# Hybrid retention/DeltaNet/RG-LRU block: block transposes on VectorE with 128-byte runs to DRAM, retention states in four places, q norms by block sums

## Chip, cores and metric

One core of one Trainium2 chip. The metric is the device time of one execution in microseconds; every figure of before is from runs of the same kernel on the same inputs.

## The reference, cut to what matters

Two layers on one sequence of 1024 tokens, width 1024. Layer 0 mixes with four retention heads and four gated-DeltaNet heads; layer 1 with an RG-LRU; after each mixer comes a feed-forward block with a short convolution. The change is almost all in layer 0's mixer:

```python
q_r, k_r, v_r, g_r, q_d, k_d, v_d, g_d, b_d, a_d = jnp.split(hn @ w_in, split_at, axis=-1)
# retention, chunks of 128 tokens, head by head
scores = jnp.einsum('bhnid,bhnjd->bhnij', qc, kc) * dmask
kv = jnp.einsum('bhncd,bhncv->nbhdv', k_tail, vc)      # needs k and v token-major
s = s * chunk_decay + kv_n                             # the state, chunk after chunk
y = intra + q_decay @ s_prev ; y_r = _rms(y) * silu(g_r)
# DeltaNet: causal conv + silu, l2norm of q and k, triangular solve, then a scan over chunks
v_new = u_n - w_n @ s ; o = qd_n @ s + a_n @ v_new ; s = s * cd_n + kt_n.T @ v_new
y_d = rms_norm(y_d, out_gain) * silu(g_d)
h = h + concat(y_r, y_d) @ w_out
```

## The kernel before

Activations lie feature-major: 128 features on the partitions, the 1024 tokens along the row. A projection (`project`, `project_n`) is 2 halves of 512 tokens by 8 tiles of the contraction by 3 matmuls (`mm3`, lines 328 to 330: high by high, high by low and low by high parts of fp32 numbers). Each weight quarter is loaded on SyncE's queue (line 260), cast to its high part on ScalarE (line 270) and its low part taken on VectorE (line 271); a ring of 6 quarters runs ahead of TensorE. A half accumulates in one of four PSUM tiles tagged `pp`; VectorE empties it (`evac_r`, line 388, or `rot_head`'s `evac`, lines 1437 to 1440).

Around the projections the small chains are written as generators. `slot()` is called after each three matmuls of a projection, and every second slot takes one step of a lane: `gdn` (`gates`, `a_stage`, `subst`, `merge`, then `scan(n)` for the eight chunks) and `ret` (`ret_half`). `after(n, f)` puts f off by n slots. A scheduler then orders each engine's instructions in this order of writing, moving one ahead where by its own model an earlier one isn't ready; on the chip each engine, SyncE's queue too, runs its list strictly in order.

In layer 0's mixer (`_mix0`) the projections run: three k heads together, the gates, the fourth k head, four q heads (`conv_head("q", ...)`), four gates (`gate2`), four v heads, then for each retention head its q, k and v, then the last gates. What is needed token-major is turned by TensorE transposes of 128x128 blocks against `ident` into PSUM and copied from there:

- `scan`: v at line 1389, K at line 1397;
- `ret_half`: v at line 1459, k at line 1464, copied by ScalarE at lines 1461 and 1466;
- `normalise`: the output on its way back, in `post` at lines 1366 and 1367, eight slots later, with one store (line 1368).

`qnorm` sums the squares of q by matmuls with a column of ones (line 1345). `normalise` squares on ScalarE (1352), sums on VectorE (1354, 1358), takes the power on GpSimd (1359), multiplies on VectorE (1361). `ret_half`'s state alternates between two places `rs`: the update for chunk n+1 (line 1483) must wait until the output matmul of chunk n-1 (line 1478) has read the place, and stands between the output matmuls of neighbouring chunks.

In the feed-forward block, products 0 to 6 use seven operands; `store_parts` writes them to DRAM, as high and low parts (`p_dram`, "whole") or as plain numbers (`s_dram`) that `load_set` splits again (lines 840 and 841).

Of the kernel before, what the change touches and what calls it, by code (L numbers as in the profile page):

```python
# [103 lines left out]
class Block:  # L104
# [655 lines left out]
    def ffn(self, layer, gain):  # L760
# [3 lines left out]
        s_dram = self.tc.dram_tile([2, 4, 4, P, HALF], F32, name=f"sf_dram{layer}")  # L764
# [15 lines left out]
        place = {1: 0, 4: 1, 2: 2, 6: 3}  # L780
        whole = {0: 0, 1: 1, 3: 2, 5: 3}
        room = {}

        def store_parts(p, y, hi):
# [11 lines left out]
            def store_split(o, src, at):  # L796
                A.copy(halves(hi[:, at]), src)  # L797
                V.tensor_tensor(halves(lo[:, at]), src, f32(halves(hi[:, at])), ALU.subtract)
                for e, t in enumerate((hi, lo)):
                    nc.sync.dma_start(p_dram[c, whole[o], k % 4, e], f32(t[:, at]))  # L800
# [22 lines left out]
            store_split(5, v[:, :, 0], slice(HALF, T))  # L823

        def load_set(c, o):

            x = self.operand(o)
            if o in whole:
                for k in range(4):
                    for e in range(2):  # L830
                        nc.sync.dma_start(f32(x[:, :, 4 * e + k, :]), halves(p_dram[c, whole[o], k, e]))
# [120 lines left out]
    def rglru(self, gain):  # L952
# [5 lines left out]

        sm = lambda name: pool.tile([P, 8], F32, name=name)
# [12 lines left out]
        us = pool.tile([P, 8 * HALF], F32, name="us")  # L972
        xs = pool.tile([P, 4 * T], F32R, name="xs")
# [110 lines left out]
    def mix0(self, gain):  # L1084
        tc = self.tc
        self.q_dram = tc.dram_tile([NCH, P, HALF], F32, name="q_dram")
        self.v_dram = tc.dram_tile([NCH, P, HALF], F32, name="v_dram")
# [21 lines left out]
    def _mix0(self, room):  # L1109
# [89 lines left out]
        def conv_tail(kind, h, buf, dst):  # L1199
# [9 lines left out]
            return th  # L1209

# [131 lines left out]
        def qnorm(h, s):  # L1342
            p = self.pc()
            for n in range(NCH):
                PE.matmul(p[:, n:n + 1], s[:, n * P:(n + 1) * P], self.ones, start=True, stop=True)

            V.tensor_scalar(irho[:, h * NCH:(h + 1) * NCH], p[:, 0:NCH], 4.0 * EPS, 128.0 * EPS, ALU.add, ALU.mult)

        def normalise(o, eps, ydst, i):
# [13 lines left out]
            def post():  # L1363
                p = self.pc()
                for h in range(4):
                    PE.transpose(p[:, hs(h)], on[:, hs(h)], self.ident)
                A.copy(s, p)
                nc.sync.dma_start(ydst, ps4(s) if len(ydst.shape) == 3 else s)
            self.after(8, post)

        def scan(n):
# [4 lines left out]
            nc.sync.dma_start(v, self.v_dram[n])  # L1376
# [10 lines left out]
            pv = self.pc()  # L1387
            for h in range(NH):
                PE.transpose(pv[:, hs(h)], v[:, hs(h)], self.ident)
# [3 lines left out]
            yield  # L1393
            if n < NCH - 1:
                p = self.pc()
                for h in range(NH):
                    PE.transpose(p[:, hs(h)], K[h][:, cs], self.ident)
                kt = tmp2("kt")
                V.tensor_tensor(ps4(kt), ps4(p), bc_last(cn(ekt), P), ALU.mult)
            s0, s1 = S[n % 2], S[(n + 1) % 2]  # L1400
            if n > 0:
                p = self.pc()
                for h in range(NH):
                    PE.matmul(p[:, hs(h)], K[h][:, cs], s0[:, hs(h)], start=True, stop=True)
                for h in range(NH):
                    V.scalar_tensor_tensor(v[:, hs(h)], p[:, hs(h)], col(ck, h, n), v[:, hs(h)], ALU.mult, ALU.add)
# [22 lines left out]
            normalise(o, cn(irho), self.y_dram[4:8, :, cs].rearrange("h p c -> p h c"), 0)  # L1429


        def rot_head(ti):
# [3 lines left out]
            def evac(n, sl, ps):  # L1436
# [4 lines left out]
                G.tensor_tensor(r[:, sl], r[:, sl], t, ALU.add)  # L1441
            self.project(unit, evac)
            return r

        def ret_half(h, i, q, k, v):
# [11 lines left out]
            p = self.pc()  # L1457
            for c in range(4):
                PE.transpose(p[:, hs(c)], v[:, cs(c)], self.ident)
            vt = tmp2("rvt")  # L1460
            A.copy(vt, p)
            p = self.pc()
            for c in range(4):
                PE.transpose(p[:, hs(c)], k[:, cs(c)], self.ident)
            kt = tmp2("rkt")
            A.activation(kt, p, AF.Copy, scale=retc[:, 2 * HALF + h:2 * HALF + h + 1])
            yield
# [4 lines left out]
            yield from range(2)  # L1472
            o = self.pc()
            for c in range(4):
                n = n0 + c
                s0, s1 = rs[n % 2], rs[(n + 1) % 2]
                if n > 0:
                    PE.matmul(o[:, hs(c)], qd[:, hs(c)], s0, start=True, stop=False)
                PE.matmul(o[:, hs(c)], sc[:, hs(c)], vt[:, hs(c)], start=n == 0, stop=True)
# [4 lines left out]
            normalise(o, None, self.y_dram[h][:, sl], 1)  # L1484
# [10 lines left out]

        gdn = self.lane("gdn", 2, 0)
# [60 lines left out]
        for h in range(NH):  # L1557
# [5 lines left out]
            self.after(28, lambda h=h, q2=q2: qnorm(h, q2))  # L1563
# [3 lines left out]
        for h in range(NH):  # L1567
            v = conv_head("v", h, None)
            nc.sync.dma_start(self.v_dram[:, :, hs(h)].rearrange("n p c -> p n c"),
                              v.rearrange("p (n c) -> p n c", n=NCH))  # L1570
# [3 lines left out]
        retc = rest[:, 0:2 * HALF + 4]  # L1574
        rs = [rest[:, 2 * HALF + 4 + i * P:2 * HALF + 4 + (i + 1) * P] for i in range(2)]
        nc.scalar.dma_start(retc, I["retc"])
# [8 lines left out]
        for h in range(NH):  # L1585
            q = rot_head(h)
            k = rot_head(4 + h)
            unit = self.unit("mix_in", 8 + h)
            v = self.t()
            self.project(unit, self.evac_r(v))  # L1590
            ret += [ret_half(h, i, q, k, v) for i in range(2)]
# [117 lines left out]
```

## Time and profile before

| | us |
|---|---|
| median of 3 runs | 2199.09 (2198.58 to 2200.04) |
| the profiled execution | 2200.31 |
| its span, first to last instruction | 2198.5 |
| TensorE matmuls busy | 2176.4 (99%) |
| TensorE weight loads busy | 1819.5 (83%) |
| VectorE busy | 1696.0 (77%) |
| ScalarE busy | 1069.7 (49%) |

Layer 0's mixer fills about the first 510 us. In the views below, "PE" is TensorE, "PEld" its weight loads, "DVE" VectorE, "ACT" ScalarE, "POOL" GpSimd, "SPq" the queue of SyncE that issues nearly all transfers. A row of instruction groups has: line, engine, operation, output<-inputs, shape, count | busy us, mean ns of one | idle us just before, and what ended it. Matmuls overlap, so the mean of one is longer than its step, and busy is the union.

### The profile page before, as it was taken

What the parts mean: (1) busy time and instruction counts of PE and PEld (TensorE: products, weight loads), DVE (VectorE), ACT (ScalarE), POOL (GpSimd) and SP (SyncE); (2) the same over time, 40 slices, a digit from 0 to 9 for tenths busy, and PEclk for the clock granted to TensorE, in tenths of its full rate; (3) what the DMA queues carried; (4) which work ended last, traced back from release to release, by engine and by line L of the source; (5) the groups of instructions that cost most, each with busy time, mean ns of one, the idle gap of its engine ahead of it and who ended that gap; (6) DMA issues with size and microseconds to landing.
All of it is one profiled execution on the core that took longest, in us unless ns stands there. A gap on an engine that the chain in (4) does not pass through costs nothing.

```text
span 2198.5 us, 29909 instructions
## 1 busy us (share of the span) xinstructions
PE 2176.4 (99%) x10844; PEld 1819.5 (83%) x10844; DVE 1696.0 (77%) x2576; ACT 1069.7 (49%) x1712; POOL 80.8 (4%) x73
## 2 busy tenths in 40 slices
PE   9999999999999999999999999999999999999998
PEld 8887888887888888887888888888888888878888
DVE  6988766446899988987865677778999889878644
ACT  5334433124565555554323476765655555544321
POOL 0100111200000000000000000000000000000001
PEclk9999999999999999999999999999999999999999
DMA  4243424125234544438546211242245445375542
GB/s 173 81 141 99 128 83 145 57 79 175 63 120 167 179 153 157 163 111 287 197 160 201 82 53 63 85 147 73 101 165 171 148 173 177 115 271 178 190 165 77
DMA packets 203300, 305.34 MB, mean 139 GB/s; under 512 B 31728, under 2 KB 91408, under 8 KB 203152
## 3 DMA queue, kind: packets, MB, share of 16 engines
q1 hardware_dynamic: 202720, 301.85, 40.7%
q8 instruction: 85, 1.39, 0.3%
q10 hardware_dynamic: 432, 1.58, 0.2%
q14 instruction: 63, 0.52, 0.1%
HBM read 212.63 MB, written 90.72 MB: 138 GB/s over the span
## 4 chain that ended last, share of the span: by engine, by line
PE 89%; DMA 4%; DVE 4%; issue 2%; ACT 1%; POOL 1%; SPq 0%; POOLq 0%; DVEq 0%; ACTq 0%
PE ps L328 27%; PE ps L330 27%; PE ps L329 27%; DMA t<-sf_dram 1%; DMA t<-y_dram 1%; PE pc L433 1%; DMA s<-pf_dram 1%; DMA h<-in_xT_dram 0%; DVE wlo L271 0%; PE pc L448 0%; DVE l L1273 0%; DVE l L1271 0%; PE pc L328 0%; PE pc L330 0%; PE pc L329 0%
## 5 line engine op out<-in xcount | busy, mean ns | idle before, releaser
L328 PE MATMUL ps<-s,whi 128*128 128x512 f32 (+1 forms) x2792 | 1091.0, 392 | 3.9 <-ACT s L840 1.8
L329 PE MATMUL ps<-s,whi 128*128 128x512 f32 (+1 forms) x2792 | 1084.5, 388 | 1.0 <-DVE s L841 0.7
L330 PE MATMUL ps<-s,wlo 128*128 128x512 f32 (+1 forms) x2792 | 1083.9, 388 | 0.0
L270 ACT CAST whi<-raw 128x512 fp32r<-128x512 f32 (+1 forms) x612 | 371.5, 613 | 659.1 <-PE ps L329 515.6
L328 PEld LDWEIGHTS ps<-s,whi 128*128 128x128 f32 x2792 | 524.9, 188 | 112.5 <-ACT s L840 3.1
L330 PEld LDWEIGHTS ps<-s,wlo 128*128 128x128 f32 x2792 | 524.7, 188 | 108.1 <-DVE wlo L271 0.3
L329 PEld LDWEIGHTS ps<-s,whi 128*128 128x128 f32 x2792 | 525.2, 188 | 107.3 <-DVE s L841 1.8
L271 DVE TENSOR_TENSOR wlo<-raw,whi 128x512 fp32r<-128x512 f32 (+1 forms) x612 | 412.9, 680 | 60.8 <-ACT whi L270 57.2
L774 DVE SCALAR_TENSOR_TENSOR t<-halo,cols,t 128x1024 f32<-128x1024 f32 x176 | 222.1, 1282 | 4.8 <-ACT t L772 3.5
L747 DVE TENSOR_TENSOR halo<-ps,kept 128x512 f32<-128x512 f32 (+1 forms) x138 | 92.2, 668 | 75.5 <-PE ps L330 74.2
L757 DVE TENSOR_TENSOR h<-ps,h 128x512 f32<-128x512 f32 x112 | 77.4, 691 | 82.2 <-PE ps L330 81.9
L772 ACT ACTIVATE t<-halo,cols 128x1024 f32<-128x1024 f32 x88 | 109.7, 1246 | 16.9 <-DVE halo L747 11.6
L742 ACT COPY kept<-ps 128x512 f32<-128x512 f32 (+1 forms) x138 | 77.0, 558 | 13.3 <-PE ps L330 11.2
L498 DVE TENSOR_TENSOR h<-ps,h 128x512 f32<-128x512 f32 (+1 forms) x72 | 45.3, 631 | 43.3 <-PE ps L330 43.3
L438 POOL TENSOR_TENSOR rtok<-rtok,npow 128x4 f32<-128x4 f32 (+1 forms) x11 | 11.2, 1016 | 1722.3 <-DVE rtok L437 1668.7
L857 DVE TENSOR_TENSOR t<-t 128x1024 f32<-128x1024 f32 x44 | 53.7, 1221 | 0.0
L797 ACT CAST t<-t 128x512 fp32r<-128x512 f32 x64 | 38.1, 620 | 32.0 <-DVE t L857 30.7
L852 ACT ACTIVATE t<-t 128x1024 f32<-128x1024 f32 x44 | 46.8, 1063 | 10.1 <-DVE t L774 10.0
L416 ACT ACTIVATE t<-h 128x512 f32<-128x512 f32 (+1 forms) x49 | 27.2, 562 | 46.3 <-DVE h L498 41.5
L840 ACT CAST s<-t 128x512 fp32r<-128x512 f32 x48 | 29.5, 621 | 38.4 <-DMA t<-sf_dram 34.0
L328 PE MATMUL ps<-s,s 128*128 128x256 f32 (+1 forms) x144 | 46.2, 321 | 0.0
L329 PE MATMUL ps<-s,s 128*128 128x256 f32 (+1 forms) x144 | 45.8, 318 | 0.0
(293 smaller groups left out, 2074.5 us busy)
## 6 DMA issues: line engine op xcount, KB each, us to landing
raw<-in_ffn_up_dram SPq DMA_DIRECT2D x176, 256.0 KB, 2.7
s<-pf_dram SPq DMA_DIRECT2D x128, 256.0 KB, 5.3
pf_dram<-t SPq DMA_DIRECT2D x64, 256.0 KB, 2.6
pf_dram<-lo SPq DMA_DIRECT2D x64, 256.0 KB, 2.5
sf_dram<-t SPq DMA_DIRECT2D x64, 256.0 KB, 2.2
t<-sf_dram SPq DMA_DIRECT2D x64, 256.0 KB, 5.0
raw<-in_ffn_w_dram SPq DMA_DIRECT2D x64, 256.0 KB, 2.9
raw<-in_mix_in_dram SPq DMA_DIRECT2D x62, 256.0 KB, 2.9
```

Source lines behind the costliest of these rows:

```text
L270: self.nc.scalar.copy(hi[:, 0:w], raw[:, 0:w])
L271: eng.tensor_tensor(lo[:, 0:w], raw[:, 0:w], f32(hi[:, 0:w]), ALU.subtract)
L328: mm(ps, whi, xhi, start=start, stop=False)
L329: mm(ps, whi, xlo, start=False, stop=False)
L330: mm(ps, wlo, xhi, start=False, stop=stop)
L742: A.copy(kept[o], ps)
L747: V.tensor_tensor(dst(i, j), v(ps), v(kept[k]), ALU.add)
L757: V.tensor_tensor(h(*to[o]), ps.rearrange("p (h c) -> p h c", c=256), h(*to[o]), ALU.add)
L772: A.activation(t, buf[:, 2:2 + T], AF.Identity, scale=w(0), bias=self.col(f"ffn_cb{layer}", tile_i))
L774: V.scalar_tensor_tensor(t, buf[:, 2 + j:2 + j + T], w(j), t, ALU.mult, ALU.add)
L852: A.activation(tg, tg, AF.Silu)
L857: V.tensor_tensor(tg, tg, tv, ALU.mult)
```

## The change

1. `store_t`: VectorE transposes every 32x32 block of a tile into `room`, and four transfers write it to DRAM token-major, each of 32 partitions by 32 blocks by 32 numbers (1024 runs of 128 bytes for a 1024-token tile). Used for K and v of DeltaNet (4 + 4 tiles of 1024 tokens) and for k and v of retention (8 + 8 halves). `scan` loads K and v so turned, scales them and has one lane step less; `ret_half` finds its k and v in `rt`, loaded by `ret_load`.
2. `normalise` transposes blocks on VectorE at once, in place of `post`, and stores with 4 transfers (scan) or 16 (retention half).
3. Retention: order of units v, k, q; v goes from PSUM to a half tile; the states have four places and are all updated right after the `kv` matmuls, ahead of the output matmuls; `rt`'s second half lies in the tile `lo` of `parts`.
4. `qnorm`: block transpose of the squares, a sum on VectorE over 32 columns, four stores and four loads of single numbers through `qq_dram`, and a second sum, at once instead of 28 slots later.
5. Feed-forward: operand 5 of the first half of products (c = 0) goes to DRAM as plain numbers (one store for two, one load for two) and is split at `load_set`.
6. RG-LRU: `xs` and `us` are allocated ahead of the small columns.

```diff
-            o += [(("mix_in", i), 2) for i in (h, 4 + h, 8 + h)]
+            o += [(("mix_in", i), 2) for i in (8 + h, 4 + h, h)]
...
-        place = {1: 0, 4: 1, 2: 2, 6: 3}
-        whole = {0: 0, 1: 1, 3: 2, 5: 3}
+        place = {1: 0, 4: 1, 2: 2, 6: 3, 5: 4}
+        whole = [{0: 0, 1: 1, 3: 2}, {0: 0, 1: 1, 3: 2, 5: 3}]
...
+            if 5 in whole[c]:
+                store_split(5, v[:, :, 0], slice(HALF, T))
+            else:
+                nc.sync.dma_start(halves(s_dram[c, place[5], k % 4]), v[:, :, 0])
...
+        def store_t(dst, src, room):
+            V.transpose(room, src)
+            for a in range(4):
+                bs = slice(a * 32, (a + 1) * 32)
+                nc.sync.dma_start(dst[:, bs].rearrange("(b i) j -> i b j", i=32),
+                                  room[bs, :].rearrange("p (b j) -> p b j", j=32))
...
-        def qnorm(h, s):
-            p = self.pc()
-            for n in range(NCH):
-                PE.matmul(p[:, n:n + 1], s[:, n * P:(n + 1) * P], self.ones, start=True, stop=True)
+        def qnorm(h, s, room):
+            V.transpose(room, s)
+            V.tensor_reduce(q32, room.rearrange("p (b j) -> p b j", j=32), AX.X, ALU.add)
+            d = self.qq_dram[h]
+            for a in range(4):
+                nc.sync.dma_start(d[a].rearrange("(b i) -> i b", i=32), q32[a * 32:(a + 1) * 32, :])
+            for a in range(4):
+                nc.sync.dma_start(qx[:, a * NCH:(a + 1) * NCH], d[a].rearrange("(n p) -> p n", p=P))
+            V.tensor_reduce(rho, qx.rearrange("p (a n) -> p n a", a=4), AX.X, ALU.add)
...
-            def post():
-                p = self.pc()
-                for h in range(4):
-                    PE.transpose(p[:, hs(h)], on[:, hs(h)], self.ident)
-                A.copy(s, p)
-                nc.sync.dma_start(ydst, ps4(s) if len(ydst.shape) == 3 else s)
-            self.after(8, post)
+            V.transpose(s, on)
+            for a in range(4):
+                bs = slice(a * 32, (a + 1) * 32)
+                for d, c in ydst(a):
+                    nc.sync.dma_start(d, s[bs, c].rearrange("p (m j) -> p m j", j=32))
...
-            pv = self.pc()
-            for h in range(NH):
-                PE.transpose(pv[:, hs(h)], v[:, hs(h)], self.ident)
-            V.tensor_tensor(ps4(v), ps4(pv), bc_last(cn(cv), P), ALU.mult)
...
+                nc.sync.dma_start(kt, self.kt_dram[cs])
+                V.tensor_tensor(ps4(kt), ps4(kt), bc_last(cn(ekt), P), ALU.mult)
+            V.tensor_tensor(ps4(v), ps4(v), bc_last(cn(cv), P), ALU.mult)
...
+        def ret_load(h):
+            for i in range(2):
+                for e in range(2):
+                    nc.sync.dma_start(ps4(rt[i][e]),
+                                      self.rt_dram[e, h, i * HALF:(i + 1) * HALF].rearrange("(c p) d -> p c d", p=P))
+                nc.scalar.activation(rt[i][1], rt[i][1], AF.Copy, scale=ktail[:, h:h + 1])
...
-                s0, s1 = rs[n % 2], rs[(n + 1) % 2]
+                s0, s1 = rs[n % 4], rs[(n + 1) % 4]
...
-            self.after(28, lambda h=h, q2=q2: qnorm(h, q2))
+            qnorm(h, q2, blocks())
+            store_t(self.kt_dram[:, hs(h)], K[h], blocks())
...
+            self.project(self.unit("mix_in", 8 + h), evac)
+            k = rot_head(4 + h, self.rt_dram[1, h])
             q = rot_head(h)
+            ret_load(h)
+            ret += [ret_half(h, i, q, k) for i in range(2)]
```

More of the change, by code (lines that the diff above doesn't have):

```diff
@@ L799, in store_split @@
                 for e, t in enumerate((hi, lo)):
-                    nc.sync.dma_start(p_dram[c, whole[o], k % 4, e], f32(t[:, at]))
+                    nc.sync.dma_start(p_dram[c, whole[c][o], k % 4, e], f32(t[:, at]))
             store = lambda o, r: nc.sync.dma_start(s_dram[c, place[o], k % 4], r)
@@ L1456, in ret_half @@
             yield
[L1457 to L1467, printed above, removed]
+            vt, kt = rt[i]
             kv = self.pc()
@@ L1483, in ret_half @@
                     V.scalar_tensor_tensor(s1, s0, RET_CD[h], kv[:, hs(c)], ALU.mult, ALU.add)
-            normalise(o, None, self.y_dram[h][:, sl], 1)
+            yield from range(3)
+            o = self.pc()
+            for c in range(4):
+                n = n0 + c
+                if n > 0:
+                    PE.matmul(o[:, hs(c)], qd[:, hs(c)], rs[n % 4], start=True, stop=False)
+                PE.matmul(o[:, hs(c)], sc[:, hs(c)], vt[:, hs(c)], start=n == 0, stop=True)
+            y = self.y_dram[h].rearrange("(b i) t -> i b t", i=32)
+            normalise(o, None, lambda a: [(y[:, :, (n0 + c) * P + a * 32:(n0 + c) * P + (a + 1) * 32], hs(c))
+                                          for c in range(4)], 1)
         def together(*gens):
@@ L1494, in together @@
                 yield from range(2)
+        blocks = lambda: f32(self.parts.tile([P, T], F32R, tag="lo", name="lo"))
+        half = lambda: self.kept.tile([P, HALF], F32, tag="kept", name="kept")
         gdn = self.lane("gdn", 2, 0)
```

84 lines of the change are left out of this document (43 added, 41 removed).

## The prediction

> **What bounds the kernel now.** I read the page first: its busy times and the chain that ended last.
>
> ```profile
> span 2198.5 us, 29909 instructions
> PE 2176.4 (99%) x10844; PEld 1819.5 (83%) x10844; DVE 1696.0 (77%) x2576; ACT 1069.7 (49%) x1712; POOL 80.8 (4%) x73
> PE 89%; DMA 4%; DVE 4%; issue 2%; ACT 1%; POOL 1%; SPq 0%; POOLq 0%; DVEq 0%; ACTq 0%
> ```
>
> TensorE sets the end: it is busy 99% of the span and holds 89% of the chain. So work taken off TensorE comes off the time unless a new wait of TensorE eats it. Where that could be is seen by stretches of layer 0's mixer (us, then busy us and count of PE, PEld, DVE, ACT, POOL, then clock, DMA share, GB/s):
>
> ```profile
> 65.00:97.00 32.00, 32.00 (x163) 26.90 (x162) 29.56 (x65) 13.04 (x21) 1.46 (x3) 1.00 0.29 92
> 97.00:144.00 47.00, 47.00 (x248) 40.27 (x248) 41.05 (x106) 21.05 (x45) 9.37 (x4) 1.00 0.41 110
> 144.00:187.00 43.00, 43.00 (x199) 35.86 (x199) 38.79 (x88) 9.45 (x12) 0.00 (x0) 1.00 0.40 141
> 246.00:366.00 120.00, 117.36 (x780) 104.64 (x779) 80.23 (x165) 42.32 (x101) 23.62 (x19) 1.00 0.35 105
> 366.00:478.00 112.00, 110.79 (x614) 94.73 (x614) 52.05 (x94) 24.43 (x40) 24.75 (x19) 1.00 0.22 75
> ```
>
> VectorE is the second engine: 87 to 92% busy from 65 to 187 us (the q heads, the gates, the substitution), 67% in the scans (246 to 366), 46% in the later retention heads. The granted clock is 1.00 throughout, so a price in us holds.
>
> **What TensorE loses.** The removed groups, and one that is only moved (the last):
>
> ```profile
> L1366 PE MATMUL pc<-ident,l 128*128 128x128 f32 x64 | 9.6, 272 | 0.0
> L1459 PE MATMUL pc<-ident,t 128*128 128x128 f32 x32 | 4.8, 272 | 0.0
> L1464 PE MATMUL pc<-ident,t 128*128 128x128 f32 x32 | 4.8, 273 | 0.0
> L1389 PE MATMUL pc<-ident,l 128*128 128x128 f32 x32 | 4.8, 273 | 0.0
> L1397 PE MATMUL pc<-ident,h 128*128 128x128 f32 x28 | 4.2, 272 | 0.0
> L1345 PE MATMUL pc<-ones,l 128*128 128x1 f32 x64 | 7.4, 245 | 0.0
> L1478 PE MATMUL pc<-l 128*128 128x128 f32 x56 | 11.3, 284 | 2.2 <-DVE l L1483 2.2
> ```
>
> Their busy time adds up to 35.6 us, the upper end, since it counts pipeline tails that lie under neighbours. The steps between starts are in the timeline (start, us, instruction, idle before):
>
> ```profile
> 249.06 0.39 PE L330 MATMUL ps<-s,wlo 128*128 128x512 f32 x1
> 249.29 0.60 PE L1397 MATMUL pc<-ident,h 128*128 128x128 f32 x4
> 249.64 0.48 PE L328 MATMUL ps<-s,whi 128*128 128x512 f32 x1
> 249.96 0.39 PE L329 MATMUL ps<-s,whi 128*128 128x512 f32 x1
> 100.45 1.84 PE L1345 MATMUL pc<-ones,l 128*128 128x1 f32 x16
> 102.15 0.49 PE L328 MATMUL ps<-s,whi 128*128 128x512 f32 x1
> 321.26 0.48 PE L328 MATMUL ps<-s,whi 128*128 128x512 f32 x1
> 322.12 0.49 PE L1478 MATMUL pc<-l 128*128 128x128 f32 x2 [0.38 <-DVE l L1483]
> ```
>
> Four transposes take 0.35 us to the next start, and the projection matmul behind them 0.32 instead of 0.23: 0.35 to 0.44 us a group. 188 transposes are 47 groups: 16.5 to 20.7 us. A q norm takes 1.70 to 1.79 us, four of them 6.8 to 7.2. Together 23 to 28; I take 26, since some groups stand beside other small matmuls and leave the switch behind. With four places and all updates ahead of the output matmuls, the wait of line 1478 goes: 2.2 us idle, but where 0.38 us idle is shown the matmul before held on 0.54 longer than its 0.32, so 3 us. Next late there would be the `kv` matmuls, on `rt`'s loads. **All hidden: 29 us.**
>
> **What VectorE gets.** The nearest rows for a transpose or sum of 1024 or 512 columns:
>
> ```profile
> L1205 DVE SCALAR_TENSOR_TENSOR t<-halo,cols,t 128x1024 f32<-128x1024 f32 x33 | 42.0, 1278 | 2.1 <-ACT t L1203 1.9
> L1236 DVE TENSOR_REDUCE l<-l 128x4 f32<-128x512 f32 x8 | 5.4, 680 | 0.0
> L1277 DVE COPY l<-l 128x1024 f32<-128x1024 f32 x1 | 1.1, 1112 | 0.0
> ```
>
> No block transpose is in the trace. A copy of 1024 columns took 1.11 us, a two-input operation 1.28; a lower end is 1.1, an upper end twice the dearer row, 2.5, if blocks pass at half the rate. A transpose is one in, one out like the copy, so 1.15 for 1024 and 0.62 for 512. Added: 12 transposes of 1024 (q squares, K, v: 4 each), 32 of 512 (16 retention, 16 `normalise`), 4 sums of 1024: 12 x 1.15 + 32 x 0.62 + 4 x 1.15 = 38 us. The scans' and retention's scalings only change their source. The 24 copies of ScalarE (lines 1367 and 1461) go, on an engine with room.
>
> *In the q heads* each head brings 3 x 1.15 + 0.16 = 3.6 us, written ahead of the next head's work. How late is VectorE there already?
>
> ```profile
> L388 DVE TENSOR_TENSOR t<-ps,R x24: 681/690/692, 140.0 to 504.1; 128x512 f32<-128x512 f32 x24
> 146.77 0.40 PE L328 MATMUL ps<-s,whi 128*128 128x512 f32 x1
> 146.39 0.17 DVE L1347 TENSOR_SCALAR l<-pc 128x8 f32<-128x8 f32 x1 [2.64 <-PE pc L1345]
> ```
>
> The first gate half is emptied from 140.0 to 140.7 (the first start in its row), and TensorE takes that tile again four halves on, at 146.8: 6.1 us to spare. Three heads push the emptying out by 10.8, and TensorE, freed of three q norms, comes 5.3 earlier: it waits 10.8 + 5.3 - 6.1 = **10 us**. Behind it VectorE's own 2.64 us wait for the q norm is gone, the gate heads leave room, and the substitution is what slips. Bounds: 0, if the scheduler puts a_stage's and the transposes' pieces behind the emptying; 15, if the fourth head and the loss of SyncE's order come on top.
>
> *In the scans* VectorE gets 8 x 0.62 for outputs and about 2 heads x 6 x 0.62: 12 us on 80 in a stretch that shortens to about 107, so 87%, as in 97 to 144, where TensorE stood still nowhere. A scan has four lane steps for five, so its chain (load of v, scaling, update, solve) has less air; v's only buffer is free after the last output matmul. I take **4 us** between 0 and 12. A wait is added too: k's transposes stand in VectorE's list behind GpSimd's addition,
>
> ```profile
> L1441 POOL TENSOR_TENSOR t<-t,l 128x512 f32<-128x512 f32 x16 | 24.5, 1534 | 172.2 <-ACT h L1338 107.1 <-DVE l L1440 56.8 <-ACT l L1380 8.3
> ```
>
> and what is queued behind them, the next half's emptying, waits along: at worst 8 x 1.5 = 12 us of VectorE, of which half falls in the scans' stretch (in the 4) and half in the next. In 366 to 478 the 10 us of VectorE's added work are covered by its 54% idle.
>
> **Transfers.** Added on SyncE's queue: 96 stores for K, v and retention, 160 for outputs, 32 for q sums, 23 loads; 20 go. Rows (issue ns min/median/max; DMA engines in the whole run, then in 206.5 to 211 us, where only 128-byte runs moved: packets, MB, share):
>
> ```profile
> L1246 SPq DMA_DIRECT2D l_dram<-h x32: 302/424/1571, 99.1 to 139.6; - x32
> L831 SPq DMA_DIRECT2D s<-pf_dram x128: 517/562/1323, 1002.4 to 2044.8; - x128
> q1 hardware_dynamic: 202720, 301.85, 40.7%
> DMA packets 1042, 0.12 MB, mean 26 GB/s; under 512 B 1042, under 2 KB 1042, under 8 KB 1042
> q1 hardware_dynamic: 1042, 0.12, 18.0%
> SPq L260 <- DVE wlo L271: 94.8, 29, 13.8
> ```
>
> 4.5 us x 16 x 18.0% / 1042 is 12.4 ns a packet; over the run 0.407 x 2198.5 x 16 / 202720 is 70.6 ns, the upper end. About 98,300 new packets of 128 bytes cost 76 us of 16 engines by the near row, spread over 400 us at a share of 0.22 to 0.41: hidden. By the 70.6 they would cost 434 and not be. The q sums' 32,768 single numbers are priced alike, 25 us. Issues at 0.42 us are 291 x 0.42 = 122 us of a queue that waits up to 13.8 us for ring places anyway; the ring's 6 quarters cover that: nothing, unless the queue itself becomes the bound (below). A first-half `ret_load` waits for k's store, a unit (11 us, 48 matmuls at 0.23) after k: covered.
>
> The Trainium skill says it more sharply for small transfers: DMA: Bandwidth & Descriptors, in Specifications, has 512 B as the least for line rate and a read-modify-write below. The trace agrees on the rate (10 bytes per ns and engine against 21 over the run), but its clean row is of loads; for stores see the rival.
>
> **Feed-forward and RG-LRU.** `load_set` gets four splits more on VectorE and ScalarE and four issues fewer; TensorE's wait there is small:
>
> ```profile
> L328 PE MATMUL ps<-s,whi 128*128 128x512 f32 x2744 | 1076.7, 393 | 3.0 <-ACT s L840 1.8 <-ACT s L543 0.7 <-DVE h L757 0.2
> ```
>
> 1.8 us over both layers: 0, between -2 and +4. The new places in RG-LRU: 0; TensorE doesn't wait there, and `us` and `xs` are first written long after the old tenants are read.
>
> **Sum.** 2200.3 - 26 - 3 + 10 + 4 = 2185.3 for the profiled execution, which stands 1.2 above the median, so **2184** beside 2199.1, -0.7%.
>
> **Rivals.**
> *All is hidden* (0.24): the scheduler empties PSUM first. For it: VectorE's lag is partly order, not load. 2199.1 - 29 = 2170, between 2165 and 2174.
> *VectorE's transposes are dear* (0.10): at 2.5 us for 1024, a q head brings 2 x 2.5 + 1.15 + 0.16 = 6.3, the wait is 18.9 + 5.3 - 6.1 = 18, the scans' 20 x 1.3 = 26 us fill VectorE and cost perhaps 8: 2199 - 29 + 26 = 2196, no change. The copy's row speaks against.
> The Trainium skill, VectorE: DVE Perf Modes, Rules for kernel authors, says to transpose 128x128 on TensorE where PSUM will do, and The three transpose paths lists 311 ns for VectorE's 128x128; an estimate from that page is 8 x 0.311 = 2.5 us per 1024, this rival's price. No run here shows it yet.
> *SyncE's queue becomes the bound, slower* (0.13): from 246 to 478 us some 230 issues are added to about 75 (by the code 16 stores, 24 loads of the scans, two a weight unit). At 0.42 us that is 128 us of 210. The two-level row of 562 ns shows dearer forms; from about 0.65 us an issue (200 us) the queue is full, weights come late and TensorE waits. At 0.75: 305 x 0.75 = 229, 19 past the stretch; with the waits for VectorE's transposes in the queue (as many us again), 2184 + 38 = 2222.
> *128-byte stores cost as the mean packet* (0.03): 434 us of all engines beside a share near 0.36 over 413 us: 434 + 149 - 413 = 170 late, 2354. It decides from (1 - 0.36) x 413 x 16 / 98300 = 43 ns; the 12.4 speaks against.
> The rest (0.50) is the forecast, 2174 to 2195.
>
> **Numbers.** 0.2% (4.4 us) is about what a measurement here can tell. Faster: 0.50 + 0.24 = 0.74; the same: 0.10; slower 0.16. The range takes in all-hidden and the dear transposes: 2165 to 2204; both slower rivals are left out.
>
> **What would show it.** TensorE's idle rows near 120 to 160 us: a wait of line 328 for line 388's tile, some 10 us in all; no rows of `ident` but the norms'; the transposes at about 1.15 and 0.62 us; the 32x32x32 stores at 0.42 us an issue; lane `gdn` ending earlier than 366. It is wrong if VectorE's list puts transposes behind the emptying (then 2170), or if SyncE's queue is busy over 80% in the scans.

## The result, and the profile after

The changed kernel takes **2331.85 us** (median of 4 runs, 2329.51 to 2334.5) against 2199.57 for the kernel before in the same runs: a ratio of 1.0602, 95% interval 1.0584 to 1.0621. It is 132 us slower, and 148 us above the forecast, outside the range. Of the two slower rivals, SyncE's queue becoming the bound stopped at 2222, with 38 of the 148 us. The other, 128-byte stores at the price of the mean packet, stood nearer in number (2354), but by chance: those stores took 11.6 ns in e7, not 70.6.

The profiled execution took 2332.41 us. From its page: the span, the busy times, TensorE's busy tenths and granted clock by slice of 58 us, transfers, and the chain that ended last by engine.

```profile
span 2330.6 us, 29821 instructions
PE 2193.8 (94%) x10592; PEld 1826.6 (78%) x10592; DVE 1734.4 (74%) x2628; ACT 1055.7 (45%) x1688; POOL 80.7 (3%) x73
PE   9967996579899999999999999999999999999998
PEclk9978997789899999999999999999999999999999
DMA packets 335717, 313.60 MB, mean 135 GB/s; under 512 B 167344, under 2 KB 224976, under 8 KB 335568
q1 hardware_dynamic: 334992, 310.13, 44.3%
PE 77%; DMA 9%; DVE 6%; SPq 4%; issue 2%; ACT 1%; POOL 1%; DVEq 0%; POOLq 0%; ACTq 0%
```

TensorE fell from 99% busy to 94%, and the gaps lie in the first 11 slices, layer 0's mixer. It is busy 17.4 us longer though about 26 us of its work is gone: where it waited, its granted clock fell too, and matmuls took longer (a projection matmul 422 to 424 ns on average from 120 to 200 us, 391 to 392 in the kernel before). By stretches of 40 us (same kernel; busy time of each engine, granted clock, share of the DMA engines):

```profile
core 0: us, PE busy (x) PEld busy (x) DVE busy (x) ACT busy (x) POOL busy (x), PEclk, DMA share, GB/s
120.00:160.00 40.00, 30.09 (x128) 24.94 (x128) 24.73 (x62) 10.32 (x23) 4.55 (x2) 0.83 0.54 50
160.00:200.00 40.00, 24.58 (x96) 19.77 (x96) 23.07 (x41) 11.21 (x24) 0.00 (x0) 0.81 0.83 94
360.00:400.00 40.00, 22.59 (x121) 20.49 (x120) 20.44 (x45) 10.79 (x30) 2.39 (x2) 0.76 0.47 109
440.00:480.00 40.00, 19.87 (x86) 17.14 (x87) 19.13 (x37) 7.64 (x21) 5.34 (x5) 0.73 0.41 88
```

There are two holes: 100 to 220 us, the q heads and gates, with the DMA engines up to 83% busy; and 340 to 540 us, scans and retention, where no engine is full. VectorE is under 65% busy in all four rows, so its load as such is hardly the cause (e3 below tries it). The waits of the kernel after from 80 to 600 us (total us, times, longest):

```profile
DVE l L1370 <- DMA l<-qq_dram: 36.8, 4, 11.6
SPq L1368 <- DMA qq_dram<-l: 25.1, 10, 5.6
PE ps L328 <- DVE t L388: 20.1, 2, 11.5
SPq L1392 <- DVE l L1388: 64.7, 11, 11.4
PE pc L1427 <- DVE l L1421: 28.4, 7, 10.4
```

Read them as a chain. VectorE stands 36.8 us at the second sum of q (line 1370), whose numbers are in DRAM; the PSUM emptying behind it (388) comes late, and TensorE waits for that. SyncE's queue stands 25.1 us until the single numbers have landed that it is to load (1368), and 64.7 us at the output stores (1392) for VectorE's transposes (1388), with the next loads behind it. Lines 1427 and 1421 are the scans' own chain, and TensorE has little beside it: 11 projection matmuls from 360 to 400 us, where the kernel before ran 70 beside its scans from 300 to 340.

DeltaNet's chain is where this adds up. Transfers of the kernel before, then of the kernel after, with first and last start: the load for the triangular solve, the loads for the merges, the scans' output matmuls.

```profile
L1261 SPq DMA_DIRECT2D l<-l_dram x1: 436/436/436, 142.5 to 142.5; - x1
L1292 SPq DMA_DIRECT2D l<-t_dram x64: 303/423/1618, 186.3 to 230.5; - x64
L1428 PE MATMUL pc<-l x64: 275/275/276, 254.3 to 362.7; 128*128 128x128 f32 x64
```

```profile
L1278 SPq DMA_DIRECT2D l<-l_dram x1: 1799/1799/1799, 219.1 to 219.1; - x1
L1309 SPq DMA_DIRECT2D l<-t_dram x64: 303/430/1669, 290.5 to 331.0; - x64
L1445 PE MATMUL pc<-l x64: 274/275/421, 352.5 to 482.3; 128*128 128x128 f32 x64
```

The solve starts 77 us late, the scans 98, and they end 120 us late. The same four times in every kernel that was run with TensorE's order left to the scheduler, in order of time ("+us" is the ratio, less one, times 2199.6):

| kernel | solve's load | merges' last load | scans' outputs, first to last | +us |
|---|---|---|---|---|
| before | 142.5 | 230.5 | 254.3 to 362.7 | 0 |
| e16 no turns | 142.0 | 230.0 | 260.5 to 367.5 | -6 |
| e7 outputs | 142.2 | 230.3 | 259.9 to 375.2 | +1 |
| e6 retention | 142.2 | 230.7 | 254.9 to 367.3 | +3 |
| e11 K stored, unused | 159.6 | 254.9 | 273.1 to 370.8 | +6 |
| e17 v | 142.6 | 263.5 | 287.0 to 384.9 | +20 |
| e9 K and v, K later | 144.9 | 264.7 | 282.4 to 378.6 | +28 |
| e18 retention, outputs | 143.6 | 231.7 | 257.2 to 398.0 | +32 |
| e5 K and v | 159.5 | 277.7 | 307.4 to 401.5 | +37 |
| e2 q sums | 184.0 | 288.0 | 307.7 to 419.1 | +51 |
| e15 stores by ScalarE | 155.7 | 271.1 | 295.0 to 441.8 | +66 |
| e8 outputs later | 159.3 | 275.6 | 304.9 to 417.7 | +67 |
| e10 all but q sums, K later | 145.7 | 262.4 | 289.3 to 422.7 | +69 |
| e1 all but q sums | 158.6 | 275.0 | 304.6 to 437.4 | +86 |
| e3 sums by selection | 162.2 | 290.6 | 308.6 to 436.7 | +87 |
| e4 sums' stores only | 188.7 | 300.6 | 329.2 to 456.8 | +104 |
| e12 sums, K later | 174.7 | 325.3 | 351.0 to 481.8 | +130 |
| after | 219.1 | 331.0 | 352.5 to 482.3 | +132 |

The time follows the end of the scans: in every row it is longer by as much as the scans end late, within 13 us. Where they end up to 13 us late it costs little (e7, e11), in the later rows sometimes less than the delay (e15: 66 for 79), sometimes more (e9: 28 for 16). Different parts of the change delay different links.

### The profile page after: what moved, and what is told of

Its sections match the earlier page's. It is cut to its first block, busy times and chain, and to the rows that moved or that the text cites. A ratio compares the mean times of both kernels' runs of the same rounds, so it can differ in the third digit from the quotient of the medians.

```text
span 2330.6 us, 29821 instructions
## 1 busy us (share of the span) xinstructions
PE 2193.8 (94%) x10592; PEld 1826.6 (78%) x10592; DVE 1734.4 (74%) x2628; ACT 1055.7 (45%) x1688; POOL 80.7 (3%) x73
## 4 chain that ended last, share of the span: by engine, by line
PE 77%; DMA 9%; DVE 6%; SPq 4%; issue 2%; ACT 1%; POOL 1%; DVEq 0%; POOLq 0%; ACTq 0%
PE ps L328 24%; PE ps L329 24%; PE ps L330 24%; DMA qq_dram<-l 3%; SPq L1392 2%; DMA t<-y_dram 1%; DVE t L1213 1%; DMA l<-gc_dram 1%; DMA h<-in_xT_dram 1%; PE pc L433 1%; SPq L1225 1%; DMA rt_dram<-kept 1%; POOL ov L1384 1%; PE pc L1434 0%; DMA s<-pf_dram 0%
## 5 line engine op out<-in xcount | busy, mean ns | idle before, releaser
L742 ACT COPY kept<-ps 128x512 f32<-128x512 f32 (+1 forms) x138 | 76.9, 557 | 13.4 <-PE ps L330 11.3
L1377 ACT ACTIVATE l<-pc 128x512 f32<-128x512 f32 x16 | 9.6, 597 | 89.1 <-PE pc L1445 32.2
L844 ACT CAST s<-t 128x512 fp32r<-128x512 f32 x56 | 34.5, 621 | 31.1 <-DMA t<-sf_dram 26.4
L328 PE MATMUL ps<-s,s 128*128 128x256 f32 (+1 forms) x144 | 46.2, 320 | 0.0
```

The costliest lines, as they stand in the source:

```text
L328: mm(ps, whi, xhi, start=start, stop=False)
L742: A.copy(kept[o], ps)
```

## The experiments

Theories, in the order in which they came: **A** the q sums' trip through DRAM; **B** VectorE's added load; **C** the number of 128-byte stores and issues; **D** the parts hold up one another in SyncE's one queue; **E** retention's trip itself; **F** the late start of the solve; **G** the scans' loads or VectorE; **H** TensorE's order, which the scheduler changed; **I** data that really come late; **J** v's stores among the merges' loads. The interval of each ratio reaches at most 0.0025 to either side.

**The q norms.** e1 is the kernel after with `qnorm` by matmuls as before. e2 is the kernel before with only the new `qnorm`. e3 keeps VectorE's transposes and sums and brings the numbers together by one matmul, without DRAM. e4 leaves out the 16 loads of single numbers; the norms are then made from the partial sums.

```diff
 # e2, on before: the change's qnorm, called at once
+            qnorm(h, q2, blocks())
 # e1, on after
-            qnorm(h, q2, blocks())
+            self.after(28, lambda h=h, q2=q2: qnorm(h, q2))     # qnorm as before
 # e3, on after
+                V.tensor_reduce(sel[:, k * 32:(k + 1) * 32], self.ident.rearrange("p (a i) -> p i a", a=4), AX.X, ALU.add)
+            PE.matmul(p[:, 0:P], sel, q32, start=True, stop=True)
 # e4, on after
-                nc.sync.dma_start(qx[:, a * NCH:(a + 1) * NCH], d[a].rearrange("(n p) -> p n", p=P))
-            V.tensor_reduce(rho, qx.rearrange("p (a n) -> p n a", a=4), AX.X, ALU.add)
+            V.tensor_reduce(rho, q32.rearrange("p (a n) -> p n a", a=4), AX.X, ALU.add)
```

> The changed kernel with q's norms again by matmuls with ones, 28 slots later; all else of the change stays. Theory A (the round trip of the q sums as single numbers through DRAM fills the DMA engines, holds up the stores of a_stage, so the substitution starts 76 us late and the scans 100 us late): 2175 to 2205 us, substitution from about 150 to 165 us on. Theory B (VectorE's block transposes and sums are the load): only 4 x 2.3 us of sums go, 2315 to 2330. Theory C (the number of 128-byte stores and of issues on SyncE's queue): 32 of 290 issues go, 2300 to 2325.

> The kernel before with nothing changed but q's norms (block transpose, sum on VectorE, single numbers through DRAM). Theory A: slower by most of the 132, 2270 to 2340 us. Theory B: 4 x 2.3 us more on VectorE less 7 us on TensorE, 2195 to 2210. Theory C: 2200 to 2215.

> The changed kernel with q's block transposes and sums on VectorE kept, but the sums of the four 32-feature blocks taken by one matmul with a 128x128 selection of zeros and ones for all four heads, in place of the 16 stores and 16 loads of single numbers. Theory A: 2170 to 2200 us, at or a little under the run with q norms on TensorE. Theory B: 2320 to 2335, since VectorE has all of the work. Theory C: 2300 to 2325.

> The changed kernel with the 16 loads of single numbers left out (q's norms are then taken from the wrong sums); its 16 stores of single numbers stay. Theory A in the form that the stores are at fault: 2290 to 2335 us, the stores still landing after some 13 us. If the loads, or the wait of VectorE and SyncE's queue for them, are at fault: 2180 to 2230.

Measured: e1 2290.13 (1.0392), e2 2253.32 (1.0231), e3 2290.15 (1.0394), e4 2307.74 (1.0474). The trip costs 46 us on top of the rest (1.0602 - 1.0392) and 51 alone; e3 equals e1, so VectorE's sums cost no more than the matmuls that they replace, and B falls for them. Of the 46, the stores have 18 (e4 - e1) and the loads with their waits 28. A and no other accounts for this third. The other 86 us it doesn't touch, so e1 and e3 missed every expectation, and e2 came out under A's; only e4 lies in a range, that of the stores. From 90 to 200 us, e4 and then e1:

```profile
90.00:200.00 110.00, 93.59 (x418) 76.98 (x417) 76.02 (x164) 31.15 (x60) 9.84 (x4) 0.92 0.98 100
```

```profile
90.00:200.00 110.00, 109.65 (x552) 92.78 (x551) 92.46 (x201) 36.10 (x67) 7.82 (x4) 1.00 0.51 135
```

The 16 stores of single numbers took the DMA engines' share from 0.51 to 0.98: 0.47 x 110 x 16 = 827 us. In the trace's list of packets some 320 of these are the 16,384 numbers' own, 20 ns each. Some 650 are 128-byte runs beside them, which took 44 ns each against 12 in e1; the other transfers took less. In the kernel after, nothing but the stores of single numbers moved from 91 to 98 us, and nearly nothing but the loads of them from 106 to 108:

```profile
DMA packets 3447, 0.01 MB, mean 2 GB/s; under 512 B 3447, under 2 KB 3447, under 8 KB 3447
q1 hardware_dynamic: 3447, 0.01, 103.1%
```

```profile
q1 hardware_dynamic: 1740, 0.01, 50.5%
```

That is 7 x 16 x 1.031 / 3447 = 33 ns a store and 2 x 16 x 0.505 / 1740 = 9.3 ns a load. Few packets make the stores' mean: 126 of the 3447 took over 100 ns each, the median 7. In e2, where nothing else is changed, the same two waits stand as in the kernel after:

```profile
DVE l L1354 <- DMA l<-qq_dram: 22.3, 4, 10.3
SPq L1352 <- DMA qq_dram<-l: 37.9, 12, 5.1
```

**One part alone.** On the kernel before: e5 DeltaNet's K and v turned and loaded by the scans, e6 retention's trip with its four places, e7 the outputs. e8 is e1 with the output stores issued six slots later.

```diff
 # e5, on before; scan as in the change
-            nc.sync.dma_start(v, self.v_dram[n])
+            nc.sync.dma_start(v, self.v_dram[cs])
+                nc.sync.dma_start(kt, self.kt_dram[cs])
 ...
+            store_t(self.kt_dram[:, hs(h)], K[h], blocks())
+            store_t(self.v_dram[:, hs(h)], v, blocks())
 # e6, on before; rot_head, ret_half and the loop as in the change
+            ret_load(h)
+            ret += [ret_half(h, i, q, k) for i in range(2)]
 # e7, on before; normalise and its two calls as in the change
-            self.after(8, post)
+            V.transpose(s, on)
 # e8, on e1
-            for a in range(4):
+            def post():
+                for a in range(4):
 ...
+            self.after(6, post)
```

> The kernel before with one part of the change alone: DeltaNet's k and v are transposed in blocks on VectorE and stored for the scans (kt_dram, v_dram in the new layout), which load them; everything else as before. Theory D (the three parts meet in SyncE's one queue, and each waits there behind the others' engines; a part alone costs little): 2190 to 2207, and the parts alone add up to far less than the 88 us that the kernel with all but the new q sums is slower. Rival B (VectorE's added load delays the scans) and rival C (every 128-byte store and issue has its price): the parts add up to about 88 us, and this one, with 32 of the 160 transposes' stores, has 15 to 30 of them: 2217 to 2232.

> The kernel before with one part alone: retention's v and k are transposed in blocks on VectorE, go to DRAM and come back (rt_dram), with the order v, k, q and the states in four places; q norms, DeltaNet and the outputs' transposes as before. Theory D: within 2195 to 2215, as its loads find a queue without the outputs' waits. Rival E (the trip itself is the cost: a head's loads must wait for its four stores and for the head before to be read, and weights stand behind them in the queue): 2240 to 2275, most of the 88 us alone. Rival C: 2225 to 2240.

> The kernel before with one part alone: the normalised outputs of scans and retention are transposed in blocks on VectorE and stored in 4 or 16 pieces of 128-byte rows, right behind the transpose. Theory D: this is the part that puts the longest waits on SyncE's queue (12 of 73.7 us in the kernel with all but the q sums), but what stands behind it is then only q, v and gc of the next scan and the weights: 2205 to 2235. Rival C (issues and 128-byte rows, 160 of them): 2220 to 2250. Rival E (retention's trip is the cost): 2190 to 2202.

> The whole change but the q norms (those on TensorE as before), with the output stores issued six slots later than their transposes, so that the next scan's loads stand ahead of them in SyncE's queue and the transposes are done when the queue comes to them. As many stores, issues and block transposes as in the kernel with all but the q sums (2290). Theory D: 2215 to 2260. Rivals B, C and E: no change, 2283 to 2297, since nothing but the order of the issues differs.

Measured: e5 2240.05 (1.0170), e6 2203.18 (1.0013, 1.0000 to 1.0025), e7 2201.51 (1.0006, 0.9994 to 1.0017), e8 2269.92 (1.0306). E falls: retention's trip alone is nearly free, and so are the outputs with their 160 stores, against C. The three add up to some 42 us where e1 has 86. D, as it was expected here, doesn't fit either: e5 costs more than any range had it, e7 less than D's, and e8 lies between the ranges. The later stores give back 19 of e1's: the order in the queue counts, for a part.

**When the solve starts, and the order.** e9 is e5 with K turned behind the gates, e10 is e1 so, e11 the kernel before with K turned and stored for nobody, e12 the kernel after with K and the q sums' transfers written behind the gates.

```diff
 # e9, e10: moved from the loop of the q heads to that of the gates; e11: added in that of the q heads
+            store_t(self.kt_dram[:, hs(h)], K[h], blocks())
```

> The kernel with DeltaNet's turn alone (2240), but K is turned and stored behind the four gates instead of behind the four q heads; all else is the same, so many stores and transposes too. Theory F, formed after the last runs: what costs is when DeltaNet's chain starts. The stores of the blocks for the triangular solve (l_dram) stand in SyncE's queue behind the stores of the turned K, which wait for VectorE, so the solve starts at 164 us instead of 149, the scans at 302 instead of 247, and at the end the scans have no projections left beside them. With K later the solve starts at 149 to 153, the scans by 262, and the time is 2193 to 2212. Rival G (the loads of kt and v in the scans, or the added load on VectorE, are the cost): 2233 to 2247.

> All of the change but the q norms (2290), with K turned and stored behind the gates. Theory F: the scans start by 265 and the whole takes 2185 to 2225; the 49 us that retention's trip and the outputs' turn cost in that kernel beyond DeltaNet's turn were the price of meeting late scans, as both alone were free (1.0013 and 1.0006). Rival D (the three meet in SyncE's queue whenever scans and retention run together): 2240 to 2275.

> The kernel before, with K turned and stored to DRAM behind the q heads and nobody reading it; the scans turn K and v on TensorE as before. Only the 4 transposes and 16 stores are added. Theory F: the solve starts at 160 to 168, and the time is 2220 to 2245, as with DeltaNet's whole turn. Rival G: 2197 to 2206, since 5 us of VectorE and 7 us of issues have room.

> The whole change, with K's turn and the q sums' trip through DRAM both put behind the gates (the sums themselves are taken at once and kept); all 32 transfers of single numbers are still there. Theory F: 2190 to 2235, close to the kernel with all but the q norms and K later. Rival A (the single numbers themselves are the cost, 16 stores that take 13.4 us each to land and occupy the DMA engines): 2235 to 2280, 30 us or more above that kernel.

Measured: e9 2230.96 (1.0129), e10 2269.09 (1.0312), e11 2207.98 (1.0028), e12 2332.42 (1.0591). F falls as the one cause: e9 started the solve on time and won back 9 us of 37, and e11, whose solve started 17 us late, lost only 6. Both came out between F's range and G's; e10 lies in D's; e12 is above both of its ranges. The merges make up for the difference: in e11 they are quick, in e9 not. e12 doesn't settle what position is worth, since its first store of single numbers was still issued at 91.0 us, as the scheduler moved it. But it bears on A: VectorE waits for `qq_dram` nowhere in e12, and still the trip costs 61 us (e12 less e10). From 80 to 300 us:

```profile
SPq L1263 <- DMA qq_dram<-l: 14.2, 6, 4.0
SPq L1371 <- DMA qq_dram<-l: 7.9, 3, 4.7
DVE l L1248 <- DMA l<-gc_dram: 18.4, 6, 9.3
```

SyncE's queue stands for the single numbers there too, and VectorE for other loads, of which the slowest took 14.9 us to land (5.2 in the kernel before, from 91 to 150 us). So VectorE's wait at the second sum isn't needed for the loss.

e13 and e14 are e5 and e1 with TensorE held to the order of writing, e15 is e1 with the new stores issued by ScalarE:

```diff
 # e13, e14
+            with tc.manual_schedule(engines={mybir.EngineType.PE}):
+                gd = self._mix0(...)
 # e15, in store_t and normalise
-                nc.sync.dma_start(...)
+                nc.scalar.dma_start(...)
```

> The kernel with DeltaNet's turn alone (2240), with TensorE's instructions in layer 0's mixer held in the order of writing; the other engines are ordered by the scheduler as before. In the order of writing the merges stand from the 660th and the scans from the 822nd projection matmul on, nearly as in the kernel before; the scheduler had put them behind the 819th and the 1008th. Theory H (the cost is the order: in the scheduler's model the turned K and v come late, so it spends the projections ahead of the merges and has none left beside the scans): 2195 to 2220. Rival I (the data really come late, the queue's waits are the cost, and the order only follows): TensorE now waits at the merges instead, 2235 to 2275.

> All of the change but the q norms (2290), with TensorE's instructions in layer 0's mixer in the order of writing. Theory H: 2195 to 2240. Rival I: 2275 to 2320.

> All of the change but the q norms (2290), with the new stores (turned K, v, retention's k and v, the outputs) issued by ScalarE instead of SyncE, so that SyncE's queue holds loads, the blocks for the solve and q alone; TensorE's order by the scheduler, which puts the merges behind the 662nd to 888th projection matmul, the first scan behind the 892nd. Theory D or I (SyncE's one queue couples the parts): 2215 to 2260, with some of it given back as ScalarE now waits for VectorE ahead of its casts of weights. Theory H: 2255 to 2290, as the scans keep few projections beside them.

Measured: e13 2282.42 (1.0358), e14 2300.81 (1.0451), e15 2268.78 (1.0301). H isn't borne out: with the order held both are slower. Part of that is the order of writing itself, which is 7 to 9 us late already behind the first three k heads; the kernel before wasn't run so, and how large the part is stays open. e14 lies in I's range, e13 above it. That the data are late, as I says, shows in e13 from 80 to 480 us:

```profile
PE pc L1315 <- DMA l<-t_dram: 24.1, 7, 15.5
```

e15 lies in H's range and above that of D and I, but fits no one theory well: without the new stores SyncE's queue is freer and the time 20 us less, and ScalarE, which casts the weights, now waits in its turn.

**The last two pairs.** e17 turns DeltaNet's v alone; e18 has retention and outputs without DeltaNet's turn.

```diff
 # e17, on before; K as before. e18 is e6 and e7 together
-                PE.transpose(pv[:, hs(h)], v[:, hs(h)], self.ident)
 ...
+            store_t(self.v_dram[:, hs(h)], v, blocks())
```

> The kernel before with DeltaNet's v alone turned on VectorE and loaded so by the scans; K is turned on TensorE in the scans as before. In the kernel with both (2240) the stores of the turned v stand in SyncE's queue among the loads that the merges need, and wait there for VectorE: the merges take 225 to 300 us, against 223 to 264 where K alone is stored (2208). Theory J (those stores delay the merges by some 33 us, of which the chain can lose 15 to 20 before TensorE runs out of other work): the solve at 149 us as before, the merges till 260 to 280, 2212 to 2230. Rival (the cost comes from loading kt in the scans): 2198 to 2207.

> Retention's trip and the outputs' turn together, DeltaNet and the q norms as before. Alone each cost nothing (2203 and 2202). Theory D (they hold up one another in SyncE's queue: each output waits there for VectorE, with retention's stores and loads and the next scan's loads behind it): 2225 to 2260, the 45 us that they cost beside DeltaNet's turn. Rival (they cost only where the scans are late, from DeltaNet's turn): 2198 to 2212, with the scans from 247 to 375 us.

Measured: e17 2219.72 (1.0090), e18 2231.54 (1.0145), both as J and D had it. J's reading, the merges' loads in e11, e5 and e17, and the wait of v's stores among them in e17 from 180 to 265 us:

```profile
L1301 SPq DMA_DIRECT2D l<-t_dram x64: 302/428/1746, 217.8 to 254.9; - x64
```

```profile
L1301 SPq DMA_DIRECT2D l<-t_dram x64: 303/430/1342, 217.6 to 277.7; - x64
```

```profile
L1300 SPq DMA_DIRECT2D l<-t_dram x64: 303/430/1457, 186.1 to 263.5; - x64
```

```profile
SPq L1216 <- DVE lo L1213: 15.2, 3, 8.4
```

64 loads of half a us each take 44 us in the kernel before (186.3 to 230.5 above) and 37 with only K stored, but 60 and 77 us with v's stores between them. Of e17's 33 us more, the queue stood 15.2 for VectorE at v's stores. G's loads of `kt` can't be the cause of e17's 20 us, as e17 has none; what e5 costs beyond e11 and e17 together, 11 us, may be theirs and wasn't taken apart.

D's reading is the queue's wait for a free place in the weight ring (line 260). As long as the queue waits there, it is ahead of TensorE. SyncE's waits from 240 to 480 us, of the kernel before, e6, e7 and e18:

```profile
SPq L260 <- DVE wlo L271: 63.3, 20, 13.8
SPq L260 <- DVE l L1483: 30.3, 4, 16.7
```

```profile
SPq L1217 <- DVE kept L1214: 44.6, 14, 5.7
SPq L260 <- DVE wlo L271: 23.9, 11, 5.6
```

```profile
SPq L260 <- DVE wlo L271: 52.0, 10, 14.1
SPq L1367 <- DVE l L1363: 44.9, 12, 11.4
```

```profile
SPq L1376 <- DVE l L1372: 56.5, 12, 10.8
SPq L1217 <- DVE kept L1214: 21.8, 4, 8.6
SPq L1384 <- DVE l L1399: 16.5, 3, 9.0
```

The kernel before has some 94 us of such waits for ring places, its slack. Retention's stores alone (L1217) or the outputs' alone (L1367) replace a part of it with 45 us of waits for VectorE. With both, e18 has no row of L260 in this stretch at all, nor has e1: the slack is spent, and the weights and the next scan's loads (L1384) come late. TensorE's two longest waits in e18 from 140 to 480 us are for these, 17 us:

```profile
PE ps L328 <- ACT whi L270: 9.8, 2, 7.5
PE pc L1396 <- DMA l<-v_dram: 7.2, 3, 4.5
```

There the parts stop being free. The slack says nothing of DeltaNet's chain, though: e17 has 74 us of such waits left, and e5 50.

**The rest of the change.** e16 is the kernel before with the states in four places, operand 5 as plain numbers and the RG-LRU's order, and no turn.

```diff
-            yield from range(2)
-            o = self.pc()
 ...
-                s0, s1 = rs[n % 2], rs[(n + 1) % 2]
+                s0, s1 = rs[n % 4], rs[(n + 1) % 4]      # all updates, then the output matmuls
```

> What is left of the change when every turn through DRAM and the q sums are taken out: the states of retention in four places with the updates ahead of the output matmuls, operand 5 of the feed-forward as plain numbers, the RG-LRU's tiles allocated first. The prediction had 3 us less for the states and nothing for the rest. If the traces so far are read rightly (behind the mixer the kernels with the feed-forward part gained 1.4 to 4.6 us on the kernel before): 2192 to 2198. Rival (those gains were scatter of the runs, and the 3 us come back as another wait): 2198 to 2203.

Measured: 2194.73 (12 runs) against 2201.28 (17 runs), a ratio of 0.9973 (0.9962 to 0.9983): 6 us faster, the only kernel here that beats the one before. How the 6 us divide over the three edits wasn't tried; its profiled execution took 2201 us, the upper end of its runs, and can't show it.

## Why the prediction was wrong, point by point

- **Unit prices: near.** The block transposes measured 1.24 us for 1024 columns and 0.70 to 0.71 for 512, against 1.15 and 0.62. That rules out the dear-transposes rival, with 2.5 us for 1024 columns. Rows of the kernel after:

```profile
L1388 DVE STREAM_TRANSPOSE l<-l 128x512 f32<-128x512 f32 x16 | 11.3, 709 | 0.3
L1222 DVE STREAM_TRANSPOSE lo<-h 128x1024 f32<-128x1024 f32 x4 | 5.0, 1239 | 0.0
```

The two rows make 179 ns fixed and 1.04 ns a column; by an estimate from them, 128 columns alone would take 311 ns. The Trainium skill, VectorE: DVE Perf Modes, The three transpose paths, has 311 ns for 128x128 (in bf16). So the rows agree with the page; what failed was the estimate that took eight times its figure, with the fixed part in it eight times.

- **128-byte stores: right.** From 267 to 270 us, e7 moved nearly nothing else (packets, MB, share of 16 engines):

```profile
DMA packets 2039, 0.25 MB, mean 85 GB/s; under 512 B 2039, under 2 KB 2039, under 8 KB 2039
q1 hardware_dynamic: 2039, 0.25, 49.4%
```

3 x 16 x 0.494 / 2039 is 11.6 ns a packet, against 12.4. The Trainium skill, DMA: Bandwidth & Descriptors, Specifications, names a read-modify-write below 512 B; stores of 128 bytes show no price for one beside the loads, as long as no stores of single numbers run with them.

- **The q sums' single numbers, "priced alike, 25 us", hidden: the first step that failed.** The loads were as priced, 9.3 ns each. The stores took 20 to 33 ns each and slowed the 128-byte runs beside them: 18 us of the 46 to 51 (e4). The rest came with the loads and the waits for them. `qnorm` put a wait for a trip through DRAM into VectorE's list, ahead of the PSUM emptying, and another into SyncE's queue, ahead of the solve's blocks and the weights. The working named neither what is queued behind those two waits nor how long they are. The first isn't needed for the loss (e12); how the rest divides among the waits stays open.
- **Issues "nothing, unless the queue itself becomes the bound": the second.** The issues were as priced, 0.43 us by median for the outputs, 0.49 for retention; K's were 0.63 (0.56 in e5). But the cost lies in the waits in between. The rival had this mechanism, with 38 us and 0.13. It got half of the 38 from issues at 0.75 us, which measured 0.43 to 0.63, and put as much again for the waits for VectorE's transposes, of which the output stores alone had 64.7. Its sign, a queue over 80% busy in the scans, would have cleared it: from 347 to 590 us the kernel after issues 249 transfers that take 130 us, 53%. A queue that stands still counts as idle. And the trace of before had a direct measure of the slack, the waits at line 260 that are quoted above; they weren't set against the new ones.
- **K and v, "+4 for the scans": the third, a link that wasn't looked at.** The stores of K stand ahead of the solve's blocks, those of v among the merges' loads, and both delay a chain that has little to spare: 8 us at its end cost 6 in e11. The prediction expected lane `gdn` to end earlier than 366; it ended near 480.
- **The q heads' wait on PSUM, 10 us: not for the reason given.** With all the transposes but without the trip (e1), the first gate's projections start 3.4 us earlier than before. Where TensorE did wait for the emptying, it was behind the second sum.
- **TensorE's 26 us and the states' 3: right as work.** The 252 matmuls are gone (10844 to 10592 in the pages), but TensorE waits out their time and more; the states' edit is in e16's 6 us.
- **Feed-forward and RG-LRU, 0:** not contradicted; within e16's 6 us.

The sum of parts, by ratios: q sums 46; DeltaNet 37; retention with outputs 32; and some 17 that only all three together cost. That last remainder has been measured as the difference, its place was not settled (the edits of feed-forward and RG-LRU are in it too).

## What to carry to other kernels

Work that leaves a full engine for idle ones is not free because they are idle: it brings waits into lists that run strictly in order, and what counts is what stands behind each wait. Before adding transfers to a queue, read its slack from its own row of waits for free places, here 94 us from 240 to 480 us, and don't take it for enough: follow the latest chain (solve, merges, scans) link by link to see which of its transfers the new ones will stand in front of. Test parts together, not only alone: two that were free each (1.0013 and 1.0006) cost 32 us as a pair.

## What the runs showed of the hardware

A store of single 4-byte numbers to DRAM took 20 (e4) to 33 ns (after) of a DMA engine's time for each number, two to three times that of a 128-byte run (11.6 ns), while a load took 9.3. The 128-byte runs beside such stores rose from 12 to 44 ns each on average. A store of 1024 numbers, 4 KB, took 13.4 us to land by median in the kernel after. An issue's length went with the shape of the transfer, by median: 0.43 us for the outputs, most of them 32 partitions by 4 runs, 0.49 for 32 by 16 (retention's k and v) and 0.56 (e5) to 0.63 (after) for 32 by 32. VectorE's block transposes took 1.04 ns a column and 179 ns fixed. And TensorE's granted clock followed its work: 0.73 to 0.83 in the stretches where it was half to three quarters busy, 1.00 where it never waited, so that a wait costs again in the matmuls after it.
